# The order of a delta-rule step on TensorE: residuals emitted before the queries' products, and a conditional yield

## The chip, the cores and the metric

The kernel runs on one core of one Trainium2 chip. The metric is the device time of one execution in microseconds (us); less is better. Before the change the median of three runs is 1973.54 us (1972.09 to 1974.93).

A core has five engines with a queue of instructions each: TensorE (PE in the profile; its weight loads are listed apart as PEld), VectorE (DVE), ScalarE (ACT), GpSimd (POOL) and SyncE (SP), which issues the DMAs here. An engine takes its queue in order, and an instruction that needs another engine's result waits for a semaphore.

## The reference

One layer of an encoder over 1024 tokens and 16 learned ones ahead of them, with model width 1024, 8 heads of 128. Cut to what matters here:

```python
h = rmsnorm(h_res, norm1_w)
proj = h @ w_in          # q, k, v, z, beta, a, short-conv B, C, x, two merge gates
# branch A, per head and direction, per chunk of tokens (g is a running sum of log decays):
a   = I + strict_lower(beta * (k k^T) * decay)
u,w = solve(a, [v * beta, k * beta * exp(g)])
v_new = u - w @ S                                  # S: state, 128 x 128
o     = (q * exp(g)) @ S + ((q k^T) * decay) @ v_new
S     = S * exp(g_last) + (k * exp(g_last - g))^T @ v_new
# o_fwd + o_bwd, gated norm, projection; branch B: short convolution; merge; w_out; SwiGLU; final norm
```

The state S makes the chunks of a head a chain: a step needs the S of the step before. The kernel takes chunks of 128 tokens, so a head has 8 steps, and runs both directions in the same step (chunk i forward, chunk 7 - i backward).

## The kernel before

**Two parts.** The first part makes the input projection (`w_in`) and, inside it, everything of branch A; in the profile it is the stretch from the start to about 925 us. The second part (merge, output projection, SwiGLU, from line 1399 on) follows and isn't touched.

**The first part's work.** The projection is a long list of units, each the products of 128 columns of `w_in` with all tokens (`dense_steps`, recorded at line 328: 24 matmuls of 320 to 512 columns for a piece of tokens, three for each of 8 blocks since each f32 product is made of high and low parts). These *dense* matmuls are the background. Between them the program places the small work of four kinds of *streams*: `g_decay`, `g_norm`, `g_inv` (the inverse of `a` by blocks) and `g_scan` (the chain of steps). Jobs for VectorE alone (convolutions; `fs`, the forward substitution; small norms) wait in three lanes.

**What sets the order.** The order is planned when the program is written out, and the chip then follows it. A dictionary `T` holds the account of four engines' time: `pe(ns)` adds to TensorE's, `V(n, kind)` and `A(n)` set VectorE's and ScalarE's to the later of their own and TensorE's account and add the cost of an instruction. Each of them returns a time at which the result may be used, which holds a margin (`HOP` = 200 ns behind TensorE, `TOPE` = 370 ns behind VectorE and ScalarE). A stream is a Python generator that *yields* such a time: the planner (`run_streams`) comes back to it, between two dense matmuls, when TensorE's account has reached it. After that `pump` fills VectorE's queue with lane jobs until VectorE's account is 700 ns ahead of TensorE's. So a yield decides how many dense matmuls stand between two groups of small products, and the account of VectorE decides how many lane jobs stand ahead of an instruction of the chain.

**A step of the scan before** (`g_scan`, the loop stands in lines 847 to 914; `d` is the direction):

1. Line 853: the keys' products, K, one for each direction: `b1[:, d] = kT * S[d]`.
2. Line 856: the queries' products, Q: `b2[:, d] = qT * S[d]`. A yield follows with the time at which K's results may be used.
3. Line 863, VectorE: the residuals `r0[d] = negEG * b1[:, d] + vS`.
4. `late`, line 892: the inner products of the step before, I: `PQ * v2`. Then `outputs()` of the step before (lines 839 and 843 on VectorE and ScalarE).
5. A yield with the time at which the residuals may be used.
6. Line 871: the products with the inverse, N: `b2[:, 2 + d] = NP * r0[d]`. A yield.
7. Lines 878 and 883, ScalarE: `w[d]` and `v2[d]`, scaled copies of N's results. A yield for `w`.
8. Line 888: the updates, W: `b1[:, d] = kn * w[d]`. A yield.
9. Line 902, VectorE: the new state `S[d]`. A yield; then the next step.

In a head's first step only the forward direction has a state, so K and Q are one product each, and line 900 copies the backward direction's first state.

The costs in the account for a product of a step is 215 ns; for a residual or a state, `V(P, 1)`, 130 + 1.042 * 128 = 263 ns.

Of the kernel before, what the change touches and what calls it, by code (L numbers as in the profile page):

```python
# [48 lines left out]
def encoder_layer(ctx: ExitStack, tc: tile.TileContext, x, meta, norm1_w, w_in, w_ba,  # L49
# [15 lines left out]
    def uid(s):  # L65
        cnt["n"] += 1
        return f"{s}_{cnt['n']}"
# [27 lines left out]
    mm = nc.tensor.matmul  # L95
# [155 lines left out]
    T = {"pe": 0.0, "dve": 0.0, "act": 0.0, "pool": 0.0}  # L251

    def on(e, ns, ready=0.0):

        T[e] = max(T[e], ready, T["pe"]) + ns
        return T[e] + TOPE

    def pe(ns):
        T["pe"] += ns
        return T["pe"] + HOP  # L260

    def V(n, kind=0):
        return on("dve", (68 + 1.042 * n, 130 + 1.042 * n, 130 + 0.52 * n)[kind])

    def A(n):
        return on("act", 144 + 0.834 * n)
# [204 lines left out]
    def cs(c):  # L471
        return slice(META + c * P, META + (c + 1) * P)
# [301 lines left out]
    def g_scan(h, st_):  # L774
        nonlocal freed
        kq, vT, small, kn, NP, PQ, Pm = (st_[k] for k in ("kq", "vT", "small", "kn", "NP", "PQ", "Pm"))
        kT, qT = kq[:, 0], kq[:, 1]
# [6 lines left out]
        def newbank():  # L784
            return pss().rearrange("p (a n) -> p a n", a=4)
# [25 lines left out]
        S = [S0, None]  # L811
# [3 lines left out]
        def outputs():  # L815

            while pending:
                pending.pop(0)()

        def output(b2, c, d, sums):  # L820
            eg = eG[:, c, (h, 8 + h)[d]:(h, 8 + h)[d] + 1]
            first = c not in seen
            seen.add(c)
            if not sums:
                def copy():
                    nc.scalar.copy(oacc[c], b2[:, 2 + d])
                    A(P)
                pending.append(copy)
                return
            if first:  # L830
                nc.scalar.activation(oacc[c], b2[:, d], AF.Copy, scale=eg)
                A(P)
            else:
                nc.vector.scalar_tensor_tensor(out=oacc[c], in0=b2[:, d], scalar=eg, in1=oacc[c],
                                               op0=ALU.mult, op1=ALU.add)
                V(P, 1)

            def add_up():
                nc.vector.tensor_tensor(out=oacc[c], in0=b2[:, 2 + d], in1=oacc[c], op=ALU.add)  # L839
                V(P)  # L840
                if not first:
                    jk = dn.tile([P, P], F32, tag="jk", name=uid("jk"))
                    nc.scalar.activation(jk, oacc[c], AF.Square, accum_out=sso[:, c:c + 1])  # L843
                    on("act", 310)
            pending.append(add_up)

        for i in range(NC):
            cd = (i, NC - 1 - i)
            hd = (h, 8 + h)
            act_ = [d for d in range(2) if S[d] is not None]  # L850
            b1, b2 = newbank(), newbank()
            for d in act_:
                mm(b1[:, d], kT[:, cs(cd[d])], S[d], start=True, stop=True)
            t = pe(215 * len(act_))
            for d in act_:
                mm(b2[:, d], qT[:, cs(cd[d])], S[d], start=True, stop=True)
            pe(215 * len(act_))
            yield t
            r0 = [vS[:, cd[0]], vS[:, cd[1]]]
            for d in act_:  # L860
                c = cd[d]
                r0[d] = dn.tile([P, P], F32, tag=f"r{d}", name=uid("r0"))
                nc.vector.scalar_tensor_tensor(out=r0[d], in0=b1[:, d], scalar=negEG[:, c, hd[d]:hd[d] + 1], in1=vS[:, c],
                                               op0=ALU.mult, op1=ALU.add)
                t = V(P, 1)
            while late:
                late.pop(0)()
            outputs()
            yield t
            for d in range(2):  # L870
                mm(b2[:, 2 + d], NP[:, cd[d], d], r0[d], start=True, stop=True)  # L871
            yield pe(430)
            w = [None, None]
            v2 = [None, None]
            for d in range(2):
                c = cd[d]
                w[d] = dn.tile([P, P], F32, tag=f"w{d}", name=uid("w"))
                nc.scalar.activation(w[d], b2[:, 2 + d], AF.Copy, scale=ce[:, c, d:d + 1])  # L878
                t = A(P)
            for d in range(2):  # L880
                c = cd[d]
                v2[d] = dn.tile([P, P], F32, tag=f"v2{d}", name=uid("v2"))
                nc.scalar.activation(v2[d], b2[:, 2 + d], AF.Copy, scale=cc[:, c, d:d + 1])
                tv = A(P)
            if i < NC - 1:
                yield t
                for d in range(2):
                    mm(b1[:, d], kn[:, cd[d]], w[d], start=True, stop=True)
                t = pe(430)
            def inner(b2=b2, cd=cd, v2=v2):  # L890
                for d in range(2):
                    mm(b2[:, 2 + d], PQ[:, cd[d], d], v2[d], start=True, stop=True)
                return pe(430)
            if i < NC - 1:
                late.append(inner)
                yield t
                for d in range(2):
                    Sn = dn.tile([P, P], F32, tag=f"S{d}", name=uid("S"), bufs=2)
                    if S[d] is None:
                        nc.vector.tensor_copy(Sn, b1[:, d])  # L900
                    else:
                        nc.vector.scalar_tensor_tensor(out=Sn, in0=S[d], scalar=eGl[:, cd[d], hd[d]:hd[d] + 1],
                                                       in1=b1[:, d], op0=ALU.mult, op1=ALU.add)
                    t = V(P, 1)
                    S[d] = Sn
            else:
                yield tv
                t2 = inner()
                freed += 1
                yield t2  # L910

            for d in range(2):
                output(b2, cd[d], d, d in act_)
            yield t
# [73 lines left out]
    def start_streams():  # L988
        nonlocal ndec, nnorm, ninv, nscan
        h = ndec  # L990
        if h < H and h < freed + 2 and not decs:
            decs.append([g_decay(h, heads[h]), T["dve"] + HOP, h])
            ndec += 1
        h = nnorm
        if h < H and h < ndec and h < freed + 2 and not norms and all(k in heads[h] and heads[h][k]() for k in ("tk", "tq")):
            norms.append([g_norm(h, heads[h]), T["dve"] + HOP, h])
            nnorm += 1
        h = ninv
        if h < H and not invs and heads[h].get("normed"):
            invs.append([g_inv(h, heads[h]), T["dve"] + HOP, h])  # L1000
            ninv += 1
        h = nscan
        if h < H and not scans and heads[h].get("inverted") and "tv" in heads[h] and heads[h]["tv"]():
            scans.append([g_scan(h, heads[h]), T["dve"] + HOP, h])
            nscan += 1
# [641 lines left out]
    for n, j in enumerate(range(GH + 2, KT - 1), 2):  # L1647
        d = pair_steps(n, j)[0]
# [154 lines left out]
    t = KT - 1  # L1803
# [345 lines left out]
```

## Time and profile before

| | us |
|---|---|
| median of three runs | 1973.54 (1972.09 to 1974.93) |
| the profiled execution | 1973.36 |
| its span, first to last instruction | 1971.6 |
| TensorE busy | 1957.3 (99%), 11992 matmuls |
| VectorE busy | 1398.0 (71%) |
| ScalarE busy | 837.7 (42%) |
| GpSimd busy | 108.4 (5%) |

How to read it: a matmul's busy time is longer than its share of the stream, since the next starts while it drains; what a matmul costs is the distance from its start to the next one's start. A 128x128 f32 product of the program is recorded as two matmuls, so the pair of a step's two directions shows as x4. In a timeline row the first number is the start, the second the time from the first instruction's start to the last one's end, xN the number merged; idle time before it stands in square brackets with what ended it.

### The profile page before, as it was taken

What the parts mean: (1) busy time and instruction counts of PE and PEld (TensorE: products, weight loads), DVE (VectorE), ACT (ScalarE), POOL (GpSimd) and SP (SyncE); (2) the same over time, 40 slices, a digit from 0 to 9 for tenths busy, and PEclk for the clock granted to TensorE, in tenths of its full rate; (3) what the DMA queues carried; (4) which work ended last, traced back from release to release, by engine and by line L of the source; (5) the groups of instructions that cost most, each with busy time, mean ns of one, the idle gap of its engine ahead of it and who ended that gap; (6) DMA issues with size and microseconds to landing.
All of it is one profiled execution on the core that took longest, in us unless ns stands there. A gap on an engine that the chain in (4) does not pass through costs nothing.

```text
span 1971.6 us, 31923 instructions
## 1 busy us (share of the span) xinstructions
PE 1957.3 (99%) x11992; PEld 1719.6 (87%) x11992; DVE 1398.0 (71%) x3017; ACT 837.7 (42%) x1968; POOL 108.4 (5%) x410
## 2 busy tenths in 40 slices
PE   9999999999999999999999999999999999999998
PEld 8999999999999999888888888888888888878887
DVE  7888688888888888845954544468676765746575
ACT  6462364646464646343444211235333333324344
POOL 2011101010101010100000000000000000000000
PEclk9999999999999999999999999999999999999999
DMA  4122121212121212223246642133366654577654
GB/s 145 61 86 81 55 87 60 77 59 77 59 84 52 87 49 87 65 81 108 85 150 242 245 153 86 65 107 112 103 234 246 245 189 153 178 274 242 193 173 168
DMA packets 124704, 251.53 MB, mean 128 GB/s; under 512 B 44988, under 2 KB 46453, under 8 KB 122117
## 3 DMA queue, kind: packets, MB, share of 16 engines
q1 hardware_dynamic: 123957, 248.44, 37.8%
q8 instruction: 94, 1.54, 0.3%
q10 hardware_dynamic: 592, 1.05, 0.1%
q14 instruction: 61, 0.50, 0.1%
HBM read 181.20 MB, written 68.25 MB: 127 GB/s over the span
## 4 chain that ended last, share of the span: by engine, by line
PE 45%; DMA 3%; DVE 2%; ACT 1%; issue 0%; SPq 0%; DVEq 0%; ACTq 0%
PE pd L1446 12%; PE pe L1446 6%; PE pm L1446 4%; PE pe L2057 1%; PE pe L2055 1%; PE pe L2056 1%; PE pd L2057 1%; PE pd L2055 1%; PE pd L2056 1%; PE pe L134 1%; PE pe L135 1%; PE pd L135 1%; PE pd L134 1%; PE pe L136 1%; PE pd L136 1%; PE pm L2056 1%
## 5 line engine op out<-in xcount | busy, mean ns | idle before, releaser
L328 PE MATMUL pm<-hTh,wh 128*128 128x320 f32 (+4 forms) x1248 | 426.9, 347 | 0.3 <-ACT hTh L1096 0.2
L328 PE MATMUL pm<-hTh,wl 128*128 128x320 f32 (+4 forms) x1248 | 426.8, 347 | 0.0
L328 PE MATMUL pm<-al,wh 128*128 128x320 f32 (+4 forms) x1248 | 423.8, 345 | 0.0
L328 PEld LDWEIGHTS pm<-hTh,wh 128*128 128x128 f32 x1248 | 233.9, 188 | 10.7 <-ACT hTh L1096 0.9
L328 PEld LDWEIGHTS pm<-al,wh 128*128 128x128 f32 x1248 | 233.8, 188 | 10.7
L328 PEld LDWEIGHTS pm<-hTh,wl 128*128 128x128 f32 x1248 | 233.9, 188 | 10.2 <-POOL wl L1111 0.3
L102 DVE TENSOR_TENSOR al<-raw,ring_h 128x1024 fp32r<-128x1024 f32 x73 | 88.6, 1222 | 65.6 <-ACT ring_h L101 64.7
L101 ACT CAST ring_h<-raw 128x1024 fp32r<-128x1024 f32 x73 | 76.6, 1053 | 109.1 <-PE pe L2057 35.0
L982 DVE TENSOR_TENSOR wl<-raw,wh 128x512 fp32r<-128x512 f32 x112 | 75.3, 687 | 34.5 <-ACT wh L985 34.2
L350 DVE SCALAR_TENSOR_TENSOR kq<-ra,wc,kq 128x520 f32<-128x520 f32 x128 | 96.5, 754 | 3.5 <-ACT kq L380 2.0
L878 ACT ACTIVATE w<-pd,small 128x128 f32<-128x128 f32 x128 | 39.8, 362 | 123.4 <-PE pd L871 122.9
L483 DVE TENSOR_TENSOR tm<-fP,fN 128x135 f32<-128x135 f32 (+23 forms) x248 | 72.2, 291 | 4.8
L487 DVE TENSOR_TENSOR fP<-fP,tm 128x135 f32<-128x135 f32 (+23 forms) x248 | 71.9, 290 | 5.0
L985 ACT CAST wh<-raw 128x512 fp32r<-128x512 f32 x112 | 66.3, 624 | 3.8 <-issue 3.6
L101 ACT CAST wh<-raw 128x1024 fp32r<-128x1024 f32 x37 | 38.8, 1047 | 47.8 <-PE pe L135 10.4
L1994 ACT ACTIVATE b<-b 128x512 f32<-128x512 f32 x20 | 12.6, 632 | 101.6 <-DVE b L1412 101.6
L843 ACT ACTIVATE jk<-NP 128x128 f32<-128x128 f32 x64 | 19.9, 311 | 81.1 <-DVE NP L839 80.1
L102 DVE TENSOR_TENSOR wl<-raw,wh 128x1024 fp32r<-128x1024 f32 x37 | 45.1, 1219 | 10.2 <-ACT wh L101 10.0
L1446 PE MATMUL pd<-b_hl,wh 128*128 128x512 f32 x168 | 51.9, 390 | 0.0
L1412 DVE TENSOR_TENSOR b<-pd,b 128x512 f32<-128x512 f32 x21 | 14.5, 689 | 52.5 <-PE pd L1446 47.5
L350 DVE SCALAR_TENSOR_TENSOR vT<-ra,wc,vT 128x520 f32<-128x520 f32 x64 | 48.3, 754 | 1.4 <-ACT vT L380 0.7
L679 POOL TENSOR_TENSOR tm<-mP,mN 1x15 f32<-1x15 f32 (+7 forms) x120 | 36.9, 307 | 210.8 <-DMA mN<-ndm 202.4
(630 smaller groups left out, 4772.1 us busy)
## 6 DMA issues: line engine op xcount, KB each, us to landing
raw<-in_w_in_dram SPq DMA_DIRECT2D x72, 512.0 KB
raw<-in_w_gate_up_dram SPq DMA_DIRECT2D x44, 512.0 KB
sums<-in_w_down_dram SPq DMA_DIRECT2D x22, 512.0 KB
t_d<-sums SPq DMA_DIRECT2D x11, 1024.0 KB
raw<-s_d SPq DMA_DIRECT2D x44, 256.0 KB
raw<-t_d SPq DMA_DIRECT2D x44, 256.0 KB
act_d<-b SPq DMA_DIRECT2D x43, 256.0 KB
raw<-act_d SPq DMA_DIRECT2D x33, 256.0 KB
```

What stands on the lines that cost most here:

```text
L101: nc.scalar.copy(hi, src)
L102: nc.vector.tensor_tensor(out=lo, in0=src, in1=hi.bitcast(F32), op=ALU.subtract)
L134: mm(po[:m, :n], wh[:, k, :m], xhk[:, t0:t0 + n], start=(k == 0), stop=False)
L328: mm(po[:, :n], ww[:, k], f(k)[:, t0:t0 + n], start=i == 0, stop=i == 3 * KT - 1)
L350: nc.vector.scalar_tensor_tensor(out=acc, in0=raw[:, h0 + t:h0 + t + hn], scalar=wc[:, t, col:col + 1], in1=acc, op0=ALU.mult, op1=ALU.add)
L483: nc.vector.tensor_tensor(out=tv, in0=fP[:, 0:r, j:j + 1].broadcast_to([P, r, n]), in1=fN[:, j:j + 1, j + 1:32].broadcast_to([P, r, n]), o ...
L487: nc.vector.tensor_tensor(out=fP[:, 0:r, j + 1:32], in0=fP[:, 0:r, j + 1:32], in1=tv, op=ALU.subtract)
L878: nc.scalar.activation(w[d], b2[:, 2 + d], AF.Copy, scale=ce[:, c, d:d + 1])
L982: nc.vector.tensor_tensor(out=u[1][1][:, k], in0=u[2][:, k], in1=u[1][0][:, k].bitcast(F32), op=ALU.subtract)
L985: nc.scalar.copy(u[1][0][:, k], u[2][:, k])
L1446: mm(po, x[:, k], at(y, k), start=i == 0 and not add_to, stop=i == 11, skip_group_check=add_to)
L2056: mm(bank[t], h_[:, c], l_[:, hi], start=False, stop=False)
```

## The change

The queries' products move behind the emission of the residuals, with their 430 ns of TensorE's account; the yield between K and the residuals goes; and the yield ahead of N is made only if the residuals' time is more than 150 ns ahead of TensorE's account.

```diff
             b1, b2 = newbank(), newbank()
             for d in act_:
                 mm(b1[:, d], kT[:, cs(cd[d])], S[d], start=True, stop=True)
-            t = pe(215 * len(act_))
-            for d in act_:
-                mm(b2[:, d], qT[:, cs(cd[d])], S[d], start=True, stop=True)
             pe(215 * len(act_))
-            yield t
             r0 = [vS[:, cd[0]], vS[:, cd[1]]]
             for d in act_:
                 c = cd[d]
...
                 t = V(P, 1)
+            for d in act_:
+                mm(b2[:, d], qT[:, cs(cd[d])], S[d], start=True, stop=True)
+            pe(215 * len(act_))
             while late:
                 late.pop(0)()
             outputs()
-            yield t
+            if t > T["pe"] + 150:
+                yield t
             for d in range(2):
                 mm(b2[:, 2 + d], NP[:, cd[d], d], r0[d], start=True, stop=True)
             yield pe(430)
```

Line numbers move a little: the queries' products are line 863 after the change, and the residuals line 859.

Both programs hold the same matmuls. Of the 56 steps that have both directions' states, 17 have N directly behind I after the change, with no dense matmul between; in the other 39, one to nine dense matmuls stand there (before: three to nine in all 56). The planner answers to the accounts at each point, so from the first scan on, nearly all streams' places among the dense matmuls shift by some.

TensorE's queue at the second step of the last head's scan. `S`, `kq`, `v`, `PQ`, `r`, `NP` are the state, keys and queries, scaled copies, inner weights, residuals and inverse; `pd` is a bank of PSUM; `hTh`, `al`, `wh`, `wl` belong to the dense matmuls. Before:

```order
L853 MATMUL pd_11679<-S_11670,kq_9477 128x128
L853 MATMUL pd_11679<-S_11672,kq_9477 128x128
L856 MATMUL pd_11680<-S_11670,kq_9477 128x128
L856 MATMUL pd_11680<-S_11672,kq_9477 128x128
L892 MATMUL pd_11644<-v_1956_11659,PQ_10011 128x128
L892 MATMUL pd_11644<-v_1957_11661,PQ_10011 128x128
L328 MATMUL pm_11631<-al_126,wh_11407 128x512
L328 MATMUL pm_11631<-hTh,wl_11408 128x512
L328 MATMUL pm_11697<-hTh,wh_11407 128x512
L871 MATMUL pd_11680<-r_1962_11685,NP_10480 128x128
L871 MATMUL pd_11680<-r_1963_11687,NP_10480 128x128
```

The same place after the change:

```order
L853 MATMUL pd_11678<-S_11669,kq_9503 128x128
L853 MATMUL pd_11678<-S_11671,kq_9503 128x128
L863 MATMUL pd_11679<-S_11669,kq_9503 128x128
L863 MATMUL pd_11679<-S_11671,kq_9503 128x128
L892 MATMUL pd_11644<-v_1956_11658,PQ_10012 128x128
L892 MATMUL pd_11644<-v_1957_11660,PQ_10012 128x128
L871 MATMUL pd_11679<-r_1962_11682,NP_10435 128x128
L871 MATMUL pd_11679<-r_1963_11684,NP_10435 128x128
L328 MATMUL pm_11631<-hTh,wh_11407 128x512
```

The three dense matmuls between I and N now stand elsewhere, behind N.

VectorE's queue in the second step of the fourth head's scan, from the residuals to the new states (`fP`, `tm`, `fN`: the lane job of the forward substitution; `wl`: the low part of the next weights; `rb`: a short convolution's product). Before:

```order
L863 SCALAR_TENSOR_TENSOR r_1064_6713<-pd_6707,negEG,vS_6558 128x128
L863 SCALAR_TENSOR_TENSOR r_1065_6715<-pd_6707,negEG,vS_6558 128x128
L839 TENSOR_TENSOR NP_5067<-pd_6656,NP_5067 128x128
L982 TENSOR_TENSOR wl_6569<-raw_6290,wh_6568 128x512
L483 TENSOR_TENSOR tm_6743<-fP_6584,fN_6583 128x31
L487 TENSOR_TENSOR fP_6584<-fP_6584,tm_6743 128x31
L483 TENSOR_TENSOR tm_6746<-fP_6584,fN_6583 128x60
L487 TENSOR_TENSOR fP_6584<-fP_6584,tm_6746 128x2x30
L483 TENSOR_TENSOR tm_6752<-fP_6584,fN_6583 128x87
L487 TENSOR_TENSOR fP_6584<-fP_6584,tm_6752 128x3x29
L902 SCALAR_TENSOR_TENSOR S_6756<-S_6697,eGl,pd_6707 128x128
L902 SCALAR_TENSOR_TENSOR S_6758<-S_6699,eGl,pd_6707 128x128
```

After:

```order
L859 SCALAR_TENSOR_TENSOR r_1064_6720<-pd_6716,negEG,vS_6573 128x128
L859 SCALAR_TENSOR_TENSOR r_1065_6722<-pd_6716,negEG,vS_6573 128x128
L839 TENSOR_TENSOR NP_5066<-pd_6663,NP_5066 128x128
L438 TENSOR_TENSOR rb_6638<-pm_6657,rb_6638 128x512
L483 TENSOR_TENSOR tm_6755<-fP_6581,fN_6580 128x31
L487 TENSOR_TENSOR fP_6581<-fP_6581,tm_6755 128x31
L483 TENSOR_TENSOR tm_6760<-fP_6581,fN_6580 128x60
L487 TENSOR_TENSOR fP_6581<-fP_6581,tm_6760 128x2x30
L483 TENSOR_TENSOR tm_6770<-fP_6581,fN_6580 128x87
L487 TENSOR_TENSOR fP_6581<-fP_6581,tm_6770 128x3x29
L902 SCALAR_TENSOR_TENSOR S_6775<-S_6706,eGl,pd_6716 128x128
L902 SCALAR_TENSOR_TENSOR S_6777<-S_6708,eGl,pd_6716 128x128
```

The residuals, the sum of outputs and the same number of lane instructions stand ahead of the new states; one 128x512 operation has changed places with another.

## The prediction

> **What bounds the kernel now.** I read the page's parts 1 and 2 first: who is busy, and at which clock.
>
> ```profile
> span 1971.6 us, 31923 instructions
> PE 1957.3 (99%) x11992; PEld 1719.6 (87%) x11992; DVE 1398.0 (71%) x3017; ACT 837.7 (42%) x1968; POOL 108.4 (5%) x410
> PEclk9999999999999999999999999999999999999999
> ```
>
> TensorE leaves 14.3 us of the span, and its clock is full in all forty slices. The stretches tell where these 14.3 us lie (us from the start, length, then the engines' busy times):
>
> ```profile
> 0.00:50.00 50.00, 46.50 (x298) 42.31 (x299) 35.81 (x85) 33.54 (x74) 11.92 (x34) 1.00 0.40 143
> 260.00:350.00 90.00, 88.91 (x787) 84.84 (x786) 78.06 (x234) 48.15 (x164) 11.46 (x47) 1.00 0.22 69
> 550.00:650.00 100.00, 100.00 (x860) 96.18 (x859) 86.83 (x258) 54.39 (x180) 11.30 (x47) 1.00 0.23 67
> 1400.00:1410.00 10.00, 8.79 (x39) 6.94 (x39) 6.98 (x9) 3.25 (x5) 0.00 (x0) 1.00 0.49 166
> 1410.00:1972.00 562.00, 553.45 (x2437) 456.74 (x2435) 361.50 (x487) 210.99 (x276) 0.00 (x0) 1.00 0.60 204
> ```
>
> 3.5 us at the opening, 8.6 + 1.2 in the second part and its end, and about 1.1 us in the whole stretch of the scans, in the slice from 260 to 350. A middle head's stretch (550 to 650) has none. The waits of TensorE by line say the same:
>
> ```profile
> PE pd L98 <- POOL ident masks.py:199: 1.5, 1, 1.5
> PE pe L1446 <- ACT b L1989: 1.2, 1, 1.2
> PE pe L590 <- DVE PQ L629: 1.1, 2, 0.8
> PE pm L2056 <- DVE al L102: 0.8, 1, 0.8
> ```
>
> No line of the scan is there, nor in the three shorter rows left out. But a busy time hides short waits, since a matmul's record reaches into the next one's; so I take the distances between starts, in a step of the last head's scan:
>
> ```profile
> 878.28 0.40 PE L328 MATMUL pm<-hTh,wh 128*128 128x512 f32 x1
> 878.51 0.61 PE L853 MATMUL pd<-S,kq 128*128 128x128 f32 x4
> 878.96 0.61 PE L856 MATMUL pd<-S,kq 128*128 128x128 f32 x4
> 879.40 0.61 PE L892 MATMUL pd<-v,PQ 128*128 128x128 f32 x4
> 879.77 0.48 PE L328 MATMUL pm<-al,wh 128*128 128x512 f32 x1
> 880.09 0.39 PE L328 MATMUL pm<-hTh,wl 128*128 128x512 f32 x1
> 880.32 0.40 PE L328 MATMUL pm<-hTh,wh 128*128 128x512 f32 x1
> 880.55 0.61 PE L871 MATMUL pd<-r,NP 128*128 128x128 f32 x4
> 880.91 0.47 PE L328 MATMUL pm<-al,wh 128*128 128x512 f32 x1
> 881.23 0.39 PE L328 MATMUL pm<-hTh,wl 128*128 128x512 f32 x1
> ...
> 883.75 0.61 PE L853 MATMUL pd<-S,kq 128*128 128x128 f32 x4
> ```
>
> A dense matmul costs 0.23 us (880.09 to 880.32), K and Q 0.44 to 0.45 each, and no start is late. The chain of a head is long, but whatever it waits for, TensorE has dense matmuls to do meanwhile, down to the last head. So the first part lasts as long as its matmuls, and a change of their order can only move time by waits that it makes or ends, or if the same matmuls cost another time in another order.
>
> **The change, part by part.** *The matmuls.* Their number is the same; 17 of 56 two-directional steps now run K, Q, I, N as one group. From the rows above: from 878.28 to 880.09 stand two dense matmuls and K, Q, I: 1.81 - 0.46 = 1.35 us for twelve matmuls, 0.1125 each. From 880.32 to 881.23 stand two dense and N: 0.91 - 0.46 = 0.45 us for four, 0.1125 each. Going from dense to narrow and back costs nothing that grows with the number of groups, so one group in place of two costs the same. At most a group's sixteen matmuls fall to 0.11 each, 0.04 us of gain a time, 17 * 0.04 = 0.7 us. Bounds -0.7 and 0; I take 0, because the two groups agree to the last digit.
>
> The Trainium skill, TensorE: Matmul & The Clock Gate, section Back-to-back issue gap, speaks against longer narrow groups: in a stream of weight loads and matmuls the spacing at 128 columns is about 81 ns, against about 56 ns for a matmul by itself, because both operations set it. If a narrow matmul next to a dense one were the cheap kind and one inside a group the dear one, merging would add an estimated 17 * 4 * 25 ns = 1.7 us. The trace disagrees, 0.1125 us in the group of four and in that of twelve.
>
> *The residuals in a merged group.* N now stands behind I, and waits if the residuals are late. VectorE beside that step:
>
> ```profile
> 879.16 0.61 DVE L863 SCALAR_TENSOR_TENSOR r<-pd,negEG,vS 128x128 f32<-128x128 f32 x2 [1.05 <-PE pd L853]
> ```
>
> Here VectorE was idle and was released by K, not by Q, so emitting the residuals ahead of Q doesn't start them sooner on the chip; it changes the account alone. The second residual ends at 879.77. In a merged group N would start at 878.51 + 0.45 + 0.44 + 0.45 = 879.85, and its second product, which needs the second residual, 0.22 later at 880.07: 0.30 us behind the residual's end. How much does a handover from VectorE to TensorE need? The row to see is a step whose K did wait for the state:
>
> ```profile
> 888.76 0.39 PE L328 MATMUL pm<-hTh,wl 128*128 128x512 f32 x1
> 889.18 0.75 PE L853 MATMUL pd<-S,kq 128*128 128x128 f32 x4
> 888.17 0.69 DVE L982 TENSOR_TENSOR wl<-raw,wh 128x512 fp32r<-128x512 f32 x1 [1.13 <-ACT wh L985]
> 888.78 0.60 DVE L902 SCALAR_TENSOR_TENSOR S<-S,eGl,pd 128x128 f32<-128x128 f32 x2
> ```
>
> The two states take 0.60 together, so the first, 0.34 (the mean of L902 in the table of groups, below), ends at 889.12 and K starts 0.06 later. That leaves 0.24 us spare in a merged group with an idle VectorE.
>
> ```profile
> L902 DVE SCALAR_TENSOR_TENSOR S<-S,eGl,pd 128x128 f32<-128x128 f32 x104 | 31.5, 341 | 22.8 <-PE pd L888 22.8
> L350 DVE SCALAR_TENSOR_TENSOR kq<-ra,wc,kq 128x520 f32<-128x520 f32 x128 | 96.5, 754 | 3.5 <-ACT kq L380 2.0 <-DVE kq L350 0.5 <-DVE tm L483 0.2
> ```
>
> With a busy VectorE the condition in the code keeps N apart: the residuals' time is VectorE's account + 2 * 263 + 370, and must not pass the end of K + 860 + 150, so the account may stand at most 114 ns behind K's end, less than the 0.2 us that a residual takes to start after K anyway (878.51 + 0.45 = 878.96 to 879.16). I take 0. If the account is wrong by one whole 128x520 operation (0.75) in all 17, it is 17 * (0.75 - 0.24) = 8.7 us: the upper end, a rival below. In unmerged steps N waits for the whole time as before.
>
> *VectorE's account runs less far ahead.* Residuals were booked behind K and Q, now behind K: 430 ns earlier. `pump` may place more lane work, and the states and the next K are released earlier by the account. K's spare time is where this bites. Of 64 starts of K, ten had less than 0.26 us behind the state's end; two of these waited, the first and the last of the ten:
>
> ```profile
> 418.45 0.32 PE L328 MATMUL pm<-hTh,wh 128*128 128x336 f32 x1
> 418.60 0.74 PE L853 MATMUL pd<-S,kq 128*128 128x128 f32 x4
> 419.17 0.39 PE L856 MATMUL pd<-S,kq 128*128 128x128 f32 x2
> 418.20 0.59 DVE L902 SCALAR_TENSOR_TENSOR S<-S,eGl,pd 128x128 f32<-128x128 f32 x2
> ```
>
> K to Q took 0.57 here instead of 0.45: 0.12 us lost; at 889.18, 0.42 - 0.23 = 0.19. Does the 430 ns reach the state? Behind the residuals stands the sum of outputs (line 839), which the account can't book ahead of I's end. Booked from K + Q + 526 = 1386 ns behind K's start before; now I's end, 1290, is the later. So 96 ns are left of it, and the other eight of the ten have 0.14 to 0.25 us behind the state's end, of which the handover takes 0.06. I take 0.1 for each of the two steps that had nothing spare, 0.2 us. Bounds: 0, and ten steps by the full 0.43, 4.3 us; I stay near the low end because the second listing of the change shows the same lane work ahead of the states.
>
> *The end of the first part.* N's removed waits let the last scan end some 14 dense matmuls (3 us) sooner in TensorE's order, with the same matmuls behind it. What could be late in the second part's beginning:
>
> ```profile
> 975.18 2.88 PE L1446 MATMUL pm<-b,mB 128*128 128x512 f32 x12
> 978.12 3.03 PE L1446 MATMUL pd<-mA,mB 128*128 128x512 f32 x12
> ```
>
> 2.94 between starts for twelve matmuls that take 12 * 0.23 = 2.72 to 2.76: 0.2 us, bounds -0.2 and 0. I take 0.
>
> *Other streams' waits.* SP's DMAs and GpSimd's work are the same too, and change places with the units and streams that issue them; I cost them at nothing, since TensorE's list of waits names no DMA, and GpSimd only at the opening. The middle heads' order before lost nothing (row 550 to 650), and the heads at 260 to 350 lost 1.1 us. Reordering gives each head a new order. Bounds: -1.1 (those waits go) and four middle heads with 1.1 each, 4.4 us. I take a sixth of the upper end, 0.7, since in the trace one stretch of the scans has such waits and the others have none.
>
> Sum: 0 + 0 + 0.2 + 0 + 0.7 = +0.9 us on the profiled execution's 1973.36, which is 0.18 below the median of the runs. Forecast 1974.3 us: no change. About 0.2% (3.9 us) is what a measurement of this kernel can tell from no change.
>
> **The rivals.** *A, slower by new waits of other streams.* For: the order is planned by accounts alone, and in the trace the two waits at line 590 (1.1 us) come from just such an order. Against: the margins of 370 ns. Its time: +2 to +6, about 1977.5; beyond 3.9 us in half of it. *B, slower by residuals that come late behind a lane operation:* N waits at the head of TensorE's queue, and the dense matmuls that stood ahead of it before now wait behind it. It decides from 0.24 us of error in the account on: 8.7 us, 1982. Against it: even behind a 128x520 operation the account held before,
>
> ```profile
> 451.22 0.60 DVE L863 SCALAR_TENSOR_TENSOR r<-pd,negEG,vS 128x128 f32<-128x128 f32 x2
> 451.89 0.61 PE L871 MATMUL pd<-r,NP 128*128 128x128 f32 x4
> ```
>
> with N's second product at 452.11, 0.29 behind the residual's end at 451.82; less 0.15 for the new condition, 0.14, still over 0.06. *C, faster:* all that can be had is 0.7 + 0.3 + 0.2 + 1.1 = 2.3 us of the terms above, 1971.1, within the 0.2%; more only if a wait of the second part ended with it (1.2 us at line 1446), 1969.9, and it lies 480 us after the last scan. *D, the clock.* If the short waits between groups took the clock to one half, a dense matmul's 0.23 would be 0.46, and the 17 steps with a merged group, of 5.24 us each (K at 878.51 to K at 883.75), would cost up to 17 * 5.24 = 89 us more. Against it: idle times of 0.8 and 1.2 us left the clock full. The Trainium skill has such a case on the same page, section A second HAM failure mode: psum-queue depth-cycling, where frequent micro-idles between matmul groups make the clock swing; no row here shows it.
>
> **How the numbers follow.** No change as forecast (-0.5 to +2 us) 0.62; A 0.18, half of it beyond the bound; B 0.08; C 0.10, of which 0.07 beyond it, if the trace hides a wait I don't see; D 0.02. Slower: 0.09 + 0.08 + 0.02 = 0.19, faster 0.07, within 0.74. The range takes in C down to 1970.4 and A up to 1979.4 us, and leaves out B, D and the ends of C.
>
> **What would show it.** TensorE busy at 1957 us within 2 and the same 11992 matmuls; K to Q to I to N at 0.45 each in the 17 merged groups (right), or a gap ahead of line 871 with a residual as its releaser (B); the residuals released by K as before; new rows of TensorE's waits at lines 590, 853 or 888 (A). A merged group that waits over 0.2 us on the average would make the prediction wrong.

## The result, and the profile after

The changed kernel is slower: 1980.42 us median of 7 runs (1977.82 to 1983.54), against 1974.93 (1972.09 to 1976.74) of the kernel before in the same session; ratio 1.0031, 95% interval 1.0019 to 1.0043. The ratio is taken over all the runs and not from the two medians. The forecast was 1974.3 us with a range up to 1979.4.

The profiled execution of the changed kernel took 1982.58 us, the second longest of the seven; it is 9.2 us behind the profiled one of before, while the medians are 5.5 us apart. Its page, parts 1 and 2, and its waits of TensorE by line (us in total, times, longest us):

```profile
span 1980.9 us, 31927 instructions
PE 1964.1 (99%) x11992; PEld 1720.5 (87%) x11992; DVE 1401.6 (71%) x3017; ACT 836.3 (42%) x1968; POOL 107.4 (5%) x410
PEclk9999999999999999999999999999999999999999
...
PE pd L1446 <- DVE b L1412: 2.0, 1, 2.0
PE pd L853 <- DVE S L902: 1.7, 3, 0.6
...
PE pd L892 <- ACT v L883: 0.2, 1, 0.2
```

The same 11992 matmuls, a clock of nine tenths or more in every slice (one short stretch at half of it is told of in the last section), and a new row: the keys' products, K (line 853), wait for the state. The stretches of the scans:

```profile
260.00:350.00 90.00, 89.51 (x788) 85.00 (x787) 77.31 (x234) 47.10 (x157) 11.35 (x49) 1.00 0.22 69
550.00:650.00 100.00, 99.70 (x858) 95.12 (x857) 88.03 (x265) 53.41 (x179) 11.39 (x47) 1.00 0.20 62
450.00:550.00 100.00, 98.89 (x839) 93.38 (x837) 85.63 (x249) 49.53 (x163) 11.65 (x47) 1.00 0.24 72
650.00:750.00 100.00, 99.23 (x843) 94.25 (x843) 84.74 (x246) 51.80 (x171) 12.45 (x47) 1.00 0.24 72
```

Before, the neighbours of the stretch from 550 to 650 were busy throughout, like that one:

```profile
450.00:550.00 100.00, 100.00 (x863) 96.24 (x862) 86.96 (x260) 52.30 (x174) 11.97 (x47) 1.00 0.22 67
650.00:750.00 100.00, 100.00 (x859) 96.25 (x858) 86.89 (x260) 52.99 (x178) 11.93 (x47) 1.00 0.25 74
```

The middle heads' stretch from 550 to 650, which had no idle time before, has some now, and its neighbours have more; the one from 260 to 350 lost a little less.

Busy time hides short waits, so I counted them by the distances between starts: how much later a matmul starts than is usual behind one of the preceding one's line and shape, between 190 and 960 us. Waits ahead of the scan's own products count from 25 ns on, those ahead of other streams' small products ("other") from some 150 to 200 ns on. Waits of dense matmuls aren't in it. In us, with the number of matmul records in brackets (a step's K is four records, and a late K shows as up to three late ones):

| | K | I | N | W | other | sum |
|---|---|---|---|---|---|---|
| before | 0.49 (6) | 0.29 (6) | 0 | 0.04 (1) | 2.03 (4) | 2.85 |
| after | 4.98 (39) | 1.43 (12) | 0.88 (9) | 0.64 (9) | 1.82 (5) | 9.75 |

The sum grew by 6.9 us. The first matmul of line 1446, where the second part's products begin, started at 967.02 us before and at 974.87 after: 7.85 us later. From there to the end the two profiled runs differ by 1.4 us more; there the changed kernel has the 2.0 us wait at line 1446 in the list above, and the kernel before one of 1.2 us at the same line. So most of the loss lies in the first part, and two thirds of the growth of its waits are ahead of K. Of 64 starts of K, 13 now come 0.05 to 0.06 us behind the end of a state, in place of two (0.05 and 0.07).

What the merged groups do is seen in the last head. TensorE, then VectorE (start, time to the last one's end, idle time before in brackets):

```profile
885.70 0.39 PE L328 MATMUL pm<-hTh,wl 128*128 128x512 f32 x1
885.93 0.61 PE L853 MATMUL pd<-S,kq 128*128 128x128 f32 x4
886.37 0.61 PE L863 MATMUL pd<-S,kq 128*128 128x128 f32 x4
886.82 0.61 PE L892 MATMUL pd<-v,PQ 128*128 128x128 f32 x4
887.26 0.61 PE L871 MATMUL pd<-r,NP 128*128 128x128 f32 x4
```

```profile
886.57 0.61 DVE L859 SCALAR_TENSOR_TENSOR r<-pd,negEG,vS 128x128 f32<-128x128 f32 x2 [1.06 <-PE pd L853]
```

K, Q, I and N follow each other at 0.44 to 0.45 us, N doesn't wait, and K releases the residuals 0.64 us after its own start. None of the 17 merged groups has a wait ahead of N; the nine in the table stand in unmerged steps. The late K don't follow the merged groups either: 11 of the 13 come behind an unmerged step, and only 0.65 of the 4.98 us behind a merged one.

One of the three large waits, in a middle head. VectorE:

```profile
545.54 0.69 DVE L982 TENSOR_TENSOR wl<-raw,wh 128x512 fp32r<-128x512 f32 x1 [0.63 <-ACT wh L985]
546.15 0.30 DVE L483 TENSOR_TENSOR tm<-fP,fN 128x143 f32<-128x143 f32 x1
546.37 0.69 DVE L358 SCALAR_TENSOR_TENSOR kq<-rb,kq 128x520 f32<-128x520 f32 x1
546.98 0.30 DVE L487 TENSOR_TENSOR fP<-fP,tm 128x143 f32<-128x143 f32 x1
547.31 0.30 DVE L483 TENSOR_TENSOR tm<-fP,fN 128x140 f32<-128x140 f32 x1
547.53 0.75 DVE L350 SCALAR_TENSOR_TENSOR kq<-ra,wc,kq 128x520 f32<-128x520 f32 x1
548.20 0.60 DVE L902 SCALAR_TENSOR_TENSOR S<-S,eGl,pd 128x128 f32<-128x128 f32 x2
```

TensorE at the same time:

```profile
544.91 0.61 PE L888 MATMUL pd<-w,kn 128*128 128x128 f32 x4
...
547.62 0.34 PE L328 MATMUL pm<-al,wh 128*128 128x384 f32 x1
548.60 0.75 PE L853 MATMUL pd<-S,kq 128*128 128x128 f32 x4 [0.64 <-DVE S L902]
```

The updates W, which the states need, start at 544.91; the states start 3.29 us later, behind two operations of the short convolutions (lines 350, 358), three of the forward substitution (483, 487) and a subtraction that waited 0.63 us for ScalarE's cast. K stands at the head of TensorE's queue and waits for them. From this step's residuals to its states VectorE has 15 instructions; in the third to sixth heads of the kernel before, where these waits are now, no such stretch has more than 11.

In the kernel before, no state started more than 1.85 us behind its W (56 steps). One of the two longest, with the same kinds of lane work (TensorE, then VectorE):

```profile
544.82 0.60 PE L888 MATMUL pd<-w,kn 128*128 128x128 f32 x4
547.21 0.61 PE L853 MATMUL pd<-S,kq 128*128 128x128 f32 x4
543.30 0.68 DVE L982 TENSOR_TENSOR wl<-raw,wh 128x512 fp32r<-128x512 f32 x1
546.67 0.60 DVE L902 SCALAR_TENSOR_TENSOR S<-S,eGl,pd 128x128 f32<-128x128 f32 x2
```

The subtraction doesn't wait for its cast there, and K isn't late. After the change 16 of 56 states start over 1.9 us behind, up to 3.29.

### The profile page after: what moved, and what is told of

It is laid out like the page before. It is cut to its first block, busy times and chain, and to the rows that moved or that the text cites. A ratio compares the mean times of both kernels' runs of the same rounds, so it can differ in the third digit from the quotient of the medians.

```text
span 1980.9 us, 31927 instructions
## 1 busy us (share of the span) xinstructions
PE 1964.1 (99%) x11992; PEld 1720.5 (87%) x11992; DVE 1401.6 (71%) x3017; ACT 836.3 (42%) x1968; POOL 107.4 (5%) x410
## 4 chain that ended last, share of the span: by engine, by line
PE 54%; DMA 3%; DVE 2%; issue 0%; ACT 0%; SPq 0%; DVEq 0%; ACTq 0%
PE pd L1446 12%; PE pe L1446 6%; PE pm L1446 4%; PE pm L328 4%; PE pe L135 2%; PE pe L136 1%; PE pe L134 1%; PE pe L2055 1%; PE pe L2056 1%; PE pe L2057 1%; PE pd L2055 1%; PE pd L2056 1%; PE pd L2057 1%; PE pd L136 1%; PE pd L135 1%; PE pd L134 1%
## 5 line engine op out<-in xcount | busy, mean ns | idle before, releaser
L859 DVE SCALAR_TENSOR_TENSOR r<-pd,negEG,vS 128x128 f32<-128x128 f32 x120 | 36.6, 343 | 15.8 <-PE pd L853 15.6
```

## The experiments

The expectations below are in us on the 1973 to 1975 of the first runs; the kernel before took 1972.16 to 1973.84 beside the experiments, so the ratios are what to compare.

Three theories at first. *Booking*: the residuals are booked 430 ns earlier, so VectorE's account runs less far ahead and more lane work gets ahead of the states. *Order by chance*: the order before has hardly a wait, and any other order loses some. *Merged groups*: each costs something by itself.

**The move without the condition** (early booking, the yield ahead of N always made, no merged group). The kernel before with:

```diff
-            t = pe(215 * len(act_))
-            for d in act_:
-                mm(b2[:, d], qT[:, cs(cd[d])], S[d], start=True, stop=True)
             pe(215 * len(act_))
-            yield t
...
                 t = V(P, 1)
+            for d in act_:
+                mm(b2[:, d], qT[:, cs(cd[d])], S[d], start=True, stop=True)
+            pe(215 * len(act_))
```

> The residuals emitted and booked ahead of the queries' products, as in the change, but the yield ahead of the products with the inverse is always made (no merged group). Theory 1, the booking: residuals booked 430 ns earlier let VectorE's account run behind the engine, so the keys' products wait for the state: +4 to +6 us against before, with 4 to 5 us of waits ahead of the keys' products. Theory 2, the luck of the order: any other order than that of before puts lane work and its waits ahead of states: +2 to +7 us. Theory 3, the merged groups: none here, so within 1 us of before.

1974.68 us (1972.76 to 1979.21, 11 runs) against 1973.84; ratio 1.0005 (0.9996 to 1.0014): no change shown. Its waits did grow, ahead of K to 2.70 us (22) and of N to 1.92 (23), in all 6.28. Early booking alone isn't the loss.

**Merged groups with the old booking** (Q stays ahead of the residuals; 42 merged groups). The kernel before with:

```diff
-            yield t
+            if t > T["pe"] + 470:
+                yield t
```

> The kernel before with the conditional yield alone: queries' products ahead of the residuals and booked so, and the yield left out where the residuals' time is at most 470 ns ahead; 42 of 56 steps become merged groups. Theory 1, the booking: within 1.5 us of before, under 1.5 us of waits ahead of the keys' products. Theory 2, the luck of the order: +2 to +7 us. Theory 3, the merged groups: 42 in place of 17 of them, +10 us or more, with the waits ahead of the products with the inverse.

1977.92 us (1977.18 to 1979.65, 11 runs) against 1973.84; ratio 1.0020 (1.0011 to 1.0029). By the ratios two thirds of the change's loss, without the early booking. The waits are again ahead of K, 4.46 us (24), and ahead of I, 2.50 (12); ahead of N only 0.93 (18). So not as the third theory expected it: 42 merged groups cost 4 us and not 10 or more, and N hardly waits for the residuals.

**Another order by an unrelated number**: the margin behind VectorE and ScalarE 380 ns in the kernel before, no merged group.

```diff
-    HOP, TOPE, DEP = 200, 370, 127
+    HOP, TOPE, DEP = 200, 380, 127
```

> The kernel before with one number changed: the margin behind VectorE and ScalarE is 380 ns in place of 370, so every handover is planned with 10 ns more, and the order shifts from the first scan on. Theory 1, the booking: more margin can only be safer, within 1 us of before. Theory 2, the luck of the order: +2 to +7 us, with waits ahead of the keys' products as in the changed kernel. Theory 3: within 1 us of before.

1976.05 us (1974.89 to 1978.84, 11 runs) against 1973.84; ratio 1.0013 (1.0004 to 1.0022). Waits 6.53 us: other streams' 4.11 (10), K 1.10 (15), I 0.99 (6). By the ratio this chance order costs 2.6 us, but not the change's 6, and mostly not ahead of K.

**The low parts' subtraction on GpSimd**, to take the cast's wait off VectorE. The changed kernel with:

```diff
-            nc.vector.tensor_tensor(out=u[1][1][:, k], in0=u[2][:, k], in1=u[1][0][:, k].bitcast(F32), op=ALU.subtract)
+            nc.gpsimd.tensor_tensor(out=u[1][1][:, k], in0=u[2][:, k], in1=u[1][0][:, k].bitcast(F32), op=ALU.subtract)
```

> The changed kernel with the low parts of the weights (112 subtractions of 128x512, 76 us of VectorE, which wait there for ScalarE's casts) issued to GpSimd, booked as before, so that every engine's order is that of the changed kernel otherwise. If the states are late because such a subtraction waits for its cast at the head of VectorE's queue (the link that theories 1 and 2 share), the waits ahead of the keys' products fall from 5.0 us to under 1.5 and the time to within 2 us of before. If lane work alone makes the states late, 3.5 us of these waits or more stay, and the time stays +4 us or more.

1986.57 us (1984.76 to 1987.27, 5 runs) against 1973.84; ratio 1.0062 (1.0049 to 1.0074): slower still, waits ahead of K 5.95 us (37). This looks like a verdict against the cast, but isn't one. The same step, VectorE and then GpSimd:

```profile
547.90 1.44 DVE L483 TENSOR_TENSOR tm<-fP,fN 128x143 f32<-128x143 f32 x1
549.26 0.69 DVE L358 SCALAR_TENSOR_TENSOR kq<-rb,kq 128x520 f32<-128x520 f32 x1
549.87 1.39 DVE L487 TENSOR_TENSOR fP<-fP,tm 128x143 f32<-128x143 f32 x1
...
552.19 0.60 DVE L902 SCALAR_TENSOR_TENSOR S<-S,eGl,pd 128x128 f32<-128x128 f32 x2
```

```profile
547.88 1.29 POOL L982 TENSOR_TENSOR wl<-raw,wh 128x512 fp32r<-128x512 f32 x1 [12.27 <-ACT wh L985]
549.43 1.66 POOL L982 TENSOR_TENSOR wl<-raw,wh 128x512 fp32r<-128x512 f32 x1 [0.26 <-PE pd L888]
```

The forward substitution's operations that took 0.30 us take 1.44 and 1.39 beside GpSimd's subtractions. One delay was put in place of another, so the cast was tested again, without GpSimd.

**No wait for the cast.** The changed kernel, and for control the kernel before, with the subtraction on VectorE reading the raw weights twice:

```diff
-            nc.vector.tensor_tensor(out=u[1][1][:, k], in0=u[2][:, k], in1=u[1][0][:, k].bitcast(F32), op=ALU.subtract)
+            nc.vector.tensor_tensor(out=u[1][1][:, k], in0=u[2][:, k], in1=u[2][:, k], op=ALU.subtract)
```

> The changed kernel, with the low parts' subtraction on VectorE (line 982) reading the raw weights twice in place of the raw weights and ScalarE's cast of them, so it no longer waits for ScalarE. Left out: the low parts of w_in become zero. Every engine's order is the changed kernel's. Theory L1 (K starts late because VectorE stands still ahead of that subtraction, 0.3 and 0.6 us each time, which its account doesn't hold): the three K of 0.64 to 0.81 us late go, and with them most of the small ones; waits ahead of K from 4.98 us to below 2.5, time 1977 to 1978. Theory L2 (K starts late because the lane work ahead of the state, convolutions above all, takes longer than the account says, with or without that wait): waits ahead of K stay above 4, time 1979.5 to 1980.5. Theory M (merged groups cost by themselves, not by late states): no change, 1980.4.

> The kernel before with the low parts' subtraction reading the raw weights twice (the low parts of w_in become zero): the control of the same edit on the changed kernel, which took 3 us off. Theories L1 and L2: the kernel before has 0.5 us of waits ahead of K, so at most 0.5 us less, ratio 0.9995 to 1.0003. If it gains 2 us or more, the edit is worth that in any order, and what it took off the changed kernel says nothing on late states.

Changed: 1975.32 us (1973.13 to 1979.74, 10 runs) against 1972.54; ratio 1.0016 (1.0006 to 1.0025). Control: 1971.26 (1969.26 to 1974.55) against 1972.16; ratio 0.9995 (0.9985 to 1.0005). With the edit on both sides the change costs 1.0016 / 0.9995 = 1.0021 in place of 1.0031, about 2 us less. The intervals are 0.001 wide to either side, so the times alone don't show these 2 us; the waits do. Those ahead of K fell from 4.98 to 1.95 us (25), and the three large ones are gone. VectorE at the step shown above:

```profile
541.80 0.69 DVE L982 TENSOR_TENSOR wl<-raw 128x512 fp32r<-128x512 f32 x1
...
542.62 0.69 DVE L982 TENSOR_TENSOR wl<-raw 128x512 fp32r<-128x512 f32 x1
...
543.44 0.70 DVE L358 SCALAR_TENSOR_TENSOR kq<-rb,kq 128x520 f32<-128x520 f32 x1
...
545.28 0.60 DVE L902 SCALAR_TENSOR_TENSOR S<-S,eGl,pd 128x128 f32<-128x128 f32 x2
```

The lane work ahead of the state is the same, and K starts without a wait: the idle time ahead of the subtractions, which VectorE's account doesn't hold, is what it took to make it late there.

**Short convolutions cut.** The changed kernel and the kernel before, with the convolutions' VectorE operations on 130 columns, the account as it was:

```diff
-                nc.vector.scalar_tensor_tensor(out=acc, in0=raw[:, h0 + t:h0 + t + hn], scalar=wc[:, t, col:col + 1],
-                                               in1=acc, op0=ALU.mult, op1=ALU.add)
+                nc.vector.scalar_tensor_tensor(out=acc[:, :130], in0=raw[:, h0 + t:h0 + t + 130], scalar=wc[:, t, col:col + 1],
+                                               in1=acc[:, :130], op0=ALU.mult, op1=ALU.add)
                 V(hn, 1)
...
-            nc.vector.scalar_tensor_tensor(out=acc, in0=th[:, :hn], scalar=1.0, in1=acc, op0=ALU.add, op1=ALU.mult)
+            nc.vector.scalar_tensor_tensor(out=acc[:, :130], in0=th[:, :130], scalar=1.0, in1=acc[:, :130], op0=ALU.add, op1=ALU.mult)
```

> The changed kernel, with the short convolutions' five VectorE operations on 130 of their 520 or so columns and the account unchanged, so every engine's order is the changed kernel's. Left out: most of the short convolutions' sums. About 128 operations of 0.75 us and 32 of 0.69 us become about 0.3 us. Theories L1 and L2: VectorE has caught up when the state is due; waits ahead of K fall from 4.98 us to below 1.5, time 1975 to 1977. Theory M: the merged groups and their order are the same, so the time stays within 1 us of 1980.4.

> The kernel before with the same shortened convolutions: the control. Its waits ahead of the scan's products are 0.8 us in all. Theories L1 and L2: at most 0.8 us less, 1973 to 1974. If it gains 3 us or more, shorter convolutions are worth that in any order, and the run of the changed kernel says nothing on late states.

Changed: 1973.40 us (1971.54 to 1975.51, 10 runs) against 1972.54; ratio 1.0004 (0.9995 to 1.0014). Control: 1971.16 (1970.04 to 1974.42); ratio 0.9997 (0.9987 to 1.0006). So with light lane work the change costs 1.0004 / 0.9997 = 1.0007, some 1.4 us, in place of 6.1, with all 17 merged groups and every engine's order as they were; this fall is larger than the intervals. Waits ahead of K: 0.80 us (11). The same step, whose K doesn't wait now:

```profile
541.01 0.69 DVE L982 TENSOR_TENSOR wl<-raw,wh 128x512 fp32r<-128x512 f32 x1 [0.64 <-ACT wh L985]
...
541.84 0.29 DVE L358 SCALAR_TENSOR_TENSOR kq<-rb,kq 128x130 f32<-128x130 f32 x1
...
542.60 0.35 DVE L350 SCALAR_TENSOR_TENSOR kq<-ra,wc,kq 128x130 f32<-128x130 f32 x1
542.86 0.60 DVE L902 SCALAR_TENSOR_TENSOR S<-S,eGl,pd 128x128 f32<-128x128 f32 x2
```

The wait for the cast is still there (0.64), and does no harm without 0.8 us of convolutions behind it. This settles the place of the loss: states behind a backlog on VectorE. The merged groups by themselves cost these 1.4 us or less; by an estimate from the two intervals, some 2.5 us to either side, it may be nothing.

**More merged groups**: the changed kernel with a margin of 400 ns, 42 merged groups.

```diff
-            if t > T["pe"] + 150:
+            if t > T["pe"] + 400:
```

> The changed kernel with a margin of 400 ns in place of 150 in the condition: 42 merged groups in place of 17, residuals booked early as in the change. Theory M (a merged group costs some 0.35 us by itself): 42/17 of the loss of 6 us, 1988. Theory L (merging shortens the steps, and a shorter step leaves the state less time behind the lane work): more waits ahead of K than 5 us, but not in proportion, 1979 to 1983, and none ahead of the products with the inverse in merged groups.

1984.81 us (1982.24 to 1985.62, 4 runs) against 1972.54; ratio 1.0058 (1.0043 to 1.0073), between the two expectations. Waits 14.48 us: other streams' 5.15 (11), K 3.45 (24), N 2.83 (27), I 1.68 (10), W 1.38 (18). I had expected none ahead of N in merged groups; here all 27 stand in them. TensorE, then VectorE:

```profile
745.90 0.61 PE L892 MATMUL pd<-v,PQ 128*128 128x128 f32 x4
746.51 0.75 PE L871 MATMUL pd<-r,NP 128*128 128x128 f32 x4
```

```profile
745.51 0.68 DVE L982 TENSOR_TENSOR wl<-raw,wh 128x512 fp32r<-128x512 f32 x1
746.11 0.60 DVE L859 SCALAR_TENSOR_TENSOR r<-pd,negEG,vS 128x128 f32<-128x128 f32 x2
```

The residuals stand behind a subtraction, and N starts 0.61 us behind I in place of 0.44. So the rival of late residuals is real. In the changed kernel, at 150 ns, the condition kept it out; but it doesn't in every order: with the same 150 ns and the backlog of 600 ns below, three of 22 merged groups have such waits, 0.48 us together.

**A shorter backlog**: lane work placed only until VectorE's account is 500 or 600 ns ahead. For 500 the changed kernel with

```diff
-        while T["dve"] <= T["pe"] + 700:
+        while T["dve"] <= T["pe"] + 500:
```

for 600 the same with that number, in the changed kernel and in the kernel before.

> The changed kernel with lane work placed only until VectorE's account is 500 ns ahead of TensorE's, in place of 700. The planner then makes 33 merged groups in place of 17. If late states behind lane work are the cause, a shorter backlog means fewer of them, in spite of more merged groups: waits ahead of K below 2.5 us, time 1974 to 1977.5 on a before of 1973. If merged groups cost by their number, 33/17 of 6 us: about 1985. If any order but the one of before loses some us by chance, 1975 to 1980 with the waits at other places.

> The same with 600 ns; 22 merged groups. Late states behind lane work: waits ahead of K between those of the changed kernel (4.98 us) and those with 500 ns, about 3; time 1976 to 1979. By the number of merged groups: 22/17 of 6 us, about 1981.

> The kernel before with 600 ns; no merged group, but another order. Late states behind lane work: its waits ahead of K were 0.49 us and stay below 1; the new order may lose 1 to 3 us elsewhere, as the order with the other margin behind VectorE did: 1973 to 1976.

| | merged | K | I | N | W | other | sum | ratio (interval) |
|---|---|---|---|---|---|---|---|---|
| changed, 500 | 33 | 0.39 (8) | 1.31 | 0.24 | 1.66 | 2.37 | 5.96 | 1.0017 (1.0007 to 1.0026) |
| changed, 600 | 22 | 1.76 (17) | 0.94 | 0.84 | 1.14 | 2.70 | 7.38 | 1.0021 (1.0012 to 1.0030) |
| changed, 700 | 17 | 4.98 (39) | 1.43 | 0.88 | 0.64 | 1.82 | 9.75 | 1.0031 (1.0019 to 1.0043) |
| before, 600 | 0 | 1.72 (17) | 0.54 | 0 | 0.67 | 3.65 | 6.57 | 1.0015 (1.0005 to 1.0024) |

The medians were 1975.94, 1976.84 and, in the last row, 1975.84 us, against 1972.65. The waits ahead of K fall with the backlog, to less than the kernel before has, while the merged groups double: it isn't their number. The expectations by late states held for both, though 1.76 us is well below "about 3"; the one by chance held for 500 ns too, since its waits are now at other places. With 500 ns the middle heads' stretches have no idle time any more,

```profile
450.00:550.00 100.00, 100.00 (x859) 95.89 (x858) 87.69 (x259) 53.05 (x177) 10.83 (x47) 1.00 0.23 72
550.00:650.00 100.00, 100.00 (x857) 95.88 (x856) 87.63 (x257) 52.51 (x174) 10.87 (x47) 1.00 0.22 67
650.00:750.00 100.00, 100.00 (x860) 95.91 (x859) 87.93 (x259) 52.82 (x173) 10.77 (x47) 1.00 0.21 67
```

and yet the kernel is some 3 us slower than before. Within its 5.96 us of waits, I, W and other streams' have grown; and ahead of 190 us, outside the count, TensorE's waits by line have a new row:

```profile
PE pm L328 <- ACT kq L380: 2.6, 2, 2.0
```

So a shorter backlog removes the late states and makes other waits, here dense matmuls that wait for ScalarE to free their bank.

And my expectation for the kernel before with 600 ns was wrong: its waits ahead of K grew to 1.72 us, without merged groups and with less backlog. Why the order of before has so few waits isn't shown. No order run here beats it, and there was little to win: with light convolutions, the kernel before itself gains 0.0003 (-0.0006 to 0.0013) of its time.

## Why the prediction was wrong, by its own steps

- *The matmuls* (0): right. Same number, and K, Q, I, N at 0.44 to 0.45 us in the merged groups. The Trainium skill's back-to-back gap, weighed there at an estimated 1.7 us, doesn't show in the groups. TensorE's busy time rose to 1964.1, outside the 1957 within 2 that I named as the sign: 1.6 us are the slow matmuls of the last section, and the rest is put down to waits that matmul records cover, an estimate from the table (the K of 548.60 shows 0.64 us of idle time and starts 0.81 late).
- *The residuals in a merged group* (0): right. No wait in 17 groups. Rival B didn't occur; the run with a margin of 400 ns shows that it exists. But "in unmerged steps N waits for the whole time as before" didn't hold: the nine late N, 0.88 us, are all there, where before had none.
- *VectorE's account runs less far ahead* (0.2, bounds 0 to 4.3): **the step that failed.** Waits ahead of K grew by 4.98 - 0.49 = 4.5 us, above the upper bound. Two errors. I priced the ten starts of K that had little spare time in the trace of before, as if the other 54 would keep theirs; in the new order 13 of the 64 starts of K waited for a state, nearly all at other places. And I took the low end because one listing of the orders showed the same lane work ahead of the states. That listing is of one step; in the steps of the three large waits 15 instructions stand between residuals and states, where the kernel before has 11 at most in the same heads. What makes it dear is what the account doesn't hold: 0.3 to 0.6 us of waiting for ScalarE's casts, behind which convolutions of 0.69 and 0.75 us stand. Taking out the waits brought K's to 1.95 us, making the convolutions short brought them to 0.80.
- *The end of the first part* (0, bounds -0.2 and 0): the place I named takes 2.73 us after the change (starts at 983.03 and 985.76) in place of 2.94, so the lower bound came. It is lost in the rest.
- *Other streams' waits* (0.7, bounds -1.1 to 4.4): the other streams' own stayed near 2 us (2.03 and 1.82); but I, N and W together gained 1.14 + 0.88 + 0.60 = 2.6 us, which no term of mine priced. I's 0.23 us at one place is a wait for ScalarE's `v2`; what makes those three late wasn't tested.
- *Rival A* (+2 to +6 us, a new row of waits at 590, 853 or 888) is what came, with the row at 853, through the scan itself and not through other streams. Its time, +6.1 us by the ratio, is at its upper end. Other orders without merged groups cost +1, +2.6 and +3 us by the ratios, of which the first isn't clear of no change.
- *Rival D, the clock*: the short waits ahead of K left it full (1.00 in the stretches of the middle heads above).

What stays open: why just this order puts 16 states late. Early booking alone (2.70 us ahead of K), merging alone (4.46) and a smaller backlog in the old order (1.72) each do some of it; I know of no rule that would have told the amount ahead of time.

## What to carry to other kernels

Where a planner's accounts set the order, an edit to one step reorders everything, and an order that the trace shows nearly free of waits can mostly lose: price the reordering itself, by some runs with an unrelated number changed, before pricing the edit. Look for what the accounts leave out (here waits of VectorE for ScalarE), since long background operations in front of a chain's instruction turn each such omission into a wait of the engine that is the bound. A test that moves work to another engine can slow the first one; take the wait out by its data instead, and run the same edit on the kernel before.

## What was not expected of the hardware

*VectorE beside GpSimd.* An operation of VectorE with two SBUF inputs went from 0.30 to 1.44 us beside a 1.29 us subtraction of GpSimd that started 0.02 us earlier. The Trainium skill, SBUF — State Buffer, section Who interferes with whom, says that the two engines share a port and that an instruction of VectorE with two SBUF inputs contends with one of GpSimd that reads SBUF; the trace agrees.

*The clock after a wait of about 2 us.* In the profiled run of the changed kernel, TensorE at line 1446:

```profile
1507.67 1.52 PE L1446 MATMUL pe<-b,mB 128*128 128x512 f32 x6
1511.17 4.61 PE L1446 MATMUL pd<-b,w 128*128 128x512 f32 x12 [1.98 <-DVE b L1412]
```

Three matmuls behind the wait the distance between starts goes from 0.23 to 0.43 us, for eight matmuls, and back: about 1.6 us lost in addition. From 1512 to 1515 us the granted clock is 0.50. In the run with the subtraction on GpSimd an idle time of 1.90 us at this place was followed by eight slower ones too (0.40 to 0.57 us); in two other runs, after 1.69 us, and in the kernel before, after 1.21 us, there were none. The Trainium skill, TensorE: Matmul & The Clock Gate, section HAM oscillation — how this bites in real kernels, gives a gap of more than about 3.4 us as the one to avoid; here 1.90 and 1.98 us were enough at this place. But the length alone doesn't decide it: 2.00 us in the run with a backlog of 500 ns (line 328 in the list above, at 72 us) and 2.28 us in the changed kernel with short convolutions (at 9 us) were followed by no slow matmul. What else it takes isn't shown.
